# Normed operands for SwiGLU tiles 3 to 21, low halves and adaLN fetches on GpSimd, adaLN steps in singles

## Chip, cores and metric

The kernel runs on one core of a Trainium2 chip. The metric is the device time of one execution in microseconds; the time of a kernel is the median of its runs. The profile is of one further execution, recorded by the hardware profiler.

## What is computed

One inference step of a two-layer backbone on 384 tokens (128 context, 256 latent) of width 1024, all in float32. Each layer is a half SwiGLU feed-forward, a mixer (layer 0: DeltaNet and windowed attention; layer 1: gated linear attention), and a second half SwiGLU. Every sub-layer is normed and modulated by shift and scale, which the adaLN projection makes from a conditioning vector, one for context and one for latent tokens. The change is in the feed-forwards:

```python
def _rmsnorm(x, g):
    y = x * lax.rsqrt(jnp.mean(x * x, axis=-1, keepdims=True) + EPS)
    return y * g

def _modnorm(x, g, shift, scale):
    return _rmsnorm(x, g) * (1.0 + scale) + shift

def _ffn_half(x, mod, i, g, w_gu, w_down):          # w_gu (1024, 2*2816), w_down (2816, 1024)
    h = _modnorm(x, g, mod[:, i], mod[:, i + 1])
    gt, up = jnp.split(h @ w_gu, 2, axis=-1)
    return x + 0.5 * mod[:, i + 2] * ((silu(gt) * up) @ w_down)

def _ada(cond, w, b):                               # nine vectors of 1024 a layer
    return (jax.nn.silu(cond) @ w + b).reshape(cond.shape[0], N_MOD, 1, D_MODEL)
```

## The kernel before

All activations lie transposed: 8 rows of 128 channels, 384 tokens wide. A float32 product is made of three products of rounded operands: weight and activation are each split into a high half (a cast on ScalarE) and a low half (a subtraction on VectorE), and `products` (L189) issues low x high, high x low and high x high for each of the 8 (or up to 6) blocks of a weight tile.

A weight tile goes through `split_w`: a DMA on SP's queue into one of three `w` buffers (L174), a cast to `wh` on ScalarE (L176), a subtraction to `wl` on VectorE (L177). `wh` and `wl` have two buffers each, so one tile's halves can be made while another's are in use.

The norm before a feed-forward is folded into the tiles. `norm_tile` makes `hh` and `hl` from x times the scale alone, without the token's factor 1/rms (`rb`), as soon as a row of x is final, and two further columns hold the shift: an operand is 386 wide. After a projection `scaled` (L203, VectorE) multiplies the result in PSUM by `rb`, and the two last columns, now the shift's share of either stream, are added as a bias: on ScalarE in the SiLU (L332, once per stream), on VectorE in the product of gate and up (L337, once per stream). `rb` itself is ready some microseconds into the first tile (`end_norm`, L300).

`ffn` has two halves of 11 tiles. A tile is a gate and an up projection of 24 matmuls each, the SiLU, the product `a`, and its split into `ah` (ScalarE, L181) and `al` (VectorE, L182). After the 11 tiles come 8 down tiles, each of 33 matmuls over two weight pieces of 6 and 5 blocks (768 and 640 columns), and a `residual` into x (L305, VectorE). In the second half `after(m)` starts the next norm on each finished row. There are four feed-forwards; between the first and second runs the even mixer, between the third and fourth the odd one.

The adaLN vectors for later sub-layers are made beside the feed-forwards, on VectorE: `ada_rows` holds two sum rows per vector (one per stream) and adds eight weight rows to each, one step per row and stream (L145 the first, L147 the others; 16 steps a vector). A weight row of 512 KB is fetched by `ada_tile` (L103) on SP's queue into one of two `aw` buffers, in front of its first step. When a vector is done `ada_sum` has TensorE sum over partitions (L161), and `ada_end` copies and transposes the result into `mod` (L128). `between` draws these steps: two or three after each tile, two after a down tile of the first half, one in the second. Its `issue_after` keeps them behind the given VectorE instruction in VectorE's order. The feed-forwards make 5, 4, 4 and 1 vectors. `side` draws early weight tiles of the following mixer from tile 18 on (first and third feed-forward).

The order in each engine's queue is made by a list scheduler when the program is built: an instruction goes in when its inputs and buffers are ready, earlier program text first. So work whose inputs are ready early can move ahead of its place in the text.

## Time and profile before

| | us |
|---|---|
| median of three runs | 1720.08 |
| lowest, highest | 1715.61, 1723.51 |
| the profiled execution: its own time | 1724.06 |
| the profiled execution: span from the first to the last instruction | 1722.3 |
| TensorE matmul busy in the span | 1656.9 |
| VectorE busy | 1237.5 |
| ScalarE busy | 749.2 |
| GpSimd busy | 0.2 |

PE is TensorE's matmuls, PEld its weight loads, DVE VectorE, ACT ScalarE, POOL GpSimd, SP the engine that issues the DMAs. Busy time is the time in which an engine has an instruction in work; matmuls overlap, so a busy TensorE is not one at its peak. The chain that ended last is followed back from the last instruction: at each step to what released it. An idle time is put down to what ended it.

### The profile page before, as it was taken

What the parts mean: (1) busy time and instruction counts of PE and PEld (TensorE: products, weight loads), DVE (VectorE), ACT (ScalarE), POOL (GpSimd) and SP (SyncE); (2) the same over time, 40 slices, a digit from 0 to 9 for tenths busy, and PEclk for the clock granted to TensorE, in tenths of its full rate; (3) what the DMA queues carried; (4) which work ended last, traced back from release to release, by engine and by line L of the source; (5) the groups of instructions that cost most, each with busy time, mean ns of one, the idle gap of its engine ahead of it and who ended that gap; (6) DMA issues with size and microseconds to landing.
All of it is one profiled execution on the core that took longest, in us unless ns stands there. A gap on an engine that the chain in (4) does not pass through costs nothing.

```text
span 1722.3 us, 26237 instructions
## 1 busy us (share of the span) xinstructions
PE 1656.9 (96%) x10341; PEld 1570.9 (91%) x10341; DVE 1237.5 (72%) x2091; ACT 749.2 (44%) x1301; POOL 0.2 (0%) x4
## 2 busy tenths in 40 slices
PE   5999998999999999999999999999999999999997
PEld 3998998899888899989999998999898889999997
DVE  3887787777868768877856887786567768744554
ACT  4432343366336443323344432344655754433343
POOL 0000000000000000000000000000000000000000
PEclk8999999999999989999999999999999999999998
DMA  8566666451321226666644656574313354434332
GB/s 321 183 186 186 204 205 210 148 188 62 114 78 50 77 84 196 180 198 196 185 132 147 197 187 198 188 228 135 102 62 96 102 172 147 159 111 136 126 110 95
DMA packets 80376, 261.83 MB, mean 152 GB/s; under 512 B 9691, under 2 KB 11739, under 8 KB 80124
## 3 DMA queue, kind: packets, MB, share of 16 engines
q1 hardware_dynamic: 80252, 260.15, 47.8%
q8 instruction: 81, 1.33, 0.3%
q14 instruction: 43, 0.35, 0.1%
HBM read 255.13 MB, written 4.98 MB: 151 GB/s over the span
## 4 chain that ended last, share of the span: by engine, by line
PE 82%; DVE 10%; DMA 4%; issue 2%; ACT 2%; SPq 0%; DVEq 0%; ACTq 0%
PE acc L189 71%; DVE acc L147 3%; DVE wl L177 2%; DMA aw<-in_adaw_dram 2%; PE ada L161 1%; DVE x L305 1%; DMA w<-in_evw_dram 1%; DMA w<-in_wdn_dram 1%; PE ps L679 1%; PE ps L683 1%; PE ada L113 1%; PE ss L289 1%; PE ps L1139 1%; PE ps L647 0%; DVE ssum L276 0%
## 5 line engine op out<-in xcount | busy, mean ns | idle before, releaser
L176 ACT CAST wh<-w 128x1024 fp32r<-128x1024 f32 (+1 forms) x358 | 340.2, 951 | 683.5 <-PE acc L189 491.0
L189 PE MATMUL acc<-hh,wl 128*128 128x386 f32 x1728 | 595.3, 345 | 7.3 <-DVE wl L177 7.2
L189 PE MATMUL acc<-hl,wh 128*128 128x386 f32 x1728 | 589.6, 341 | 0.0
L189 PE MATMUL acc<-hh,wh 128*128 128x386 f32 x1728 | 587.9, 340 | 0.0
L177 DVE TENSOR_TENSOR wl<-w,wh 128x1024 fp32r<-128x1024 f32 (+1 forms) x358 | 392.3, 1097 | 98.3 <-ACT wh L176 96.8
L189 PEld LDWEIGHTS acc<-hh,wl 128*128 128x128 f32 x1728 | 325.6, 188 | 19.4 <-DVE wl L177 9.5
L189 PEld LDWEIGHTS acc<-hl,wh 128*128 128x128 f32 x1728 | 327.2, 189 | 2.3 <-issue 0.8
L189 PEld LDWEIGHTS acc<-hh,wh 128*128 128x128 f32 x1728 | 325.5, 188 | 2.3 <-issue 0.8
L189 PE MATMUL acc<-ah,wl 128*128 128x384 f32 x704 | 242.2, 344 | 17.2 <-DVE wl L177 16.8
L147 DVE SCALAR_TENSOR_TENSOR acc<-aw,cs,acc 128x1024 f32<-128x1024 f32 x196 | 243.1, 1278 | 8.4 <-DMA aw<-in_adaw_dram 8.4
L189 PE MATMUL acc<-al,wh 128*128 128x384 f32 x704 | 238.5, 339 | 0.0
L189 PE MATMUL acc<-ah,wh 128*128 128x384 f32 x704 | 238.4, 339 | 0.0
L189 PEld LDWEIGHTS acc<-ah,wl 128*128 128x128 f32 x704 | 132.7, 189 | 27.9 <-DVE wl L177 27.9
L189 PEld LDWEIGHTS acc<-al,wh 128*128 128x128 f32 x704 | 132.9, 189 | 0.0
L189 PEld LDWEIGHTS acc<-ah,wh 128*128 128x128 f32 x704 | 132.8, 189 | 0.0
L203 DVE TENSOR_TENSOR tu<-acc,rb 128x386 f32<-128x386 f32 x88 | 49.2, 559 | 105.7 <-PE acc L189 105.6
L203 DVE TENSOR_TENSOR tg<-acc,rb 128x386 f32<-128x386 f32 x138 | 76.6, 555 | 55.3 <-PE acc L189 52.0
L305 DVE SCALAR_TENSOR_TENSOR x<-acc,hg,x 128x128 f32<-128x128 f32 (+1 forms) x128 | 47.5, 413 | 68.5 <-PE acc L189 68.5
L332 ACT ACTIVATE sg<-tg 128x128 f32<-128x128 f32 (+1 forms) x176 | 70.6, 448 | 51.6 <-DVE tg L203 51.5
L337 DVE SCALAR_TENSOR_TENSOR a<-tu,sg 128x128 f32<-128x128 f32 (+1 forms) x176 | 65.7, 415 | 8.3
L181 ACT CAST ah<-a 128x384 fp32r<-128x384 f32 x88 | 45.3, 515 | 41.5 <-DVE a L337 41.3
L182 DVE TENSOR_TENSOR al<-a,ah 128x384 fp32r<-128x384 f32 x88 | 48.6, 552 | 3.5 <-ACT ah L181 3.5
(368 smaller groups left out, 1502.4 us busy)
## 6 DMA issues: line engine op xcount, KB each, us to landing
w<-in_wgu_dram SPq DMA_DIRECT2D x176, 512.0 KB, 3.7
aw<-in_adaw_dram SPq DMA_DIRECT2D x144, 512.0 KB, 4.2
w<-in_wdn_dram SPq DMA_DIRECT2D x64, 384.0 KB, 3.1
w<-in_wdn_dram SPq DMA_DIRECT2D x64, 320.0 KB, 3.0
w<-in_evw_dram SPq DMA_DIRECT2D x24, 512.0 KB, 4.1
w<-in_odw_dram SPq DMA_DIRECT2D x24, 512.0 KB, 3.6
w<-in_evo_dram SPq DMA_DIRECT2D x8, 512.0 KB, 3.5
w<-in_odo_dram SPq DMA_DIRECT2D x8, 512.0 KB, 4.0
```

Source lines behind the costliest of these rows:

```text
L113: nc.tensor.matmul(ps[32 * g:32 * g + 32, 0:256], self.cs[:, k, :], w[:, 256 * g:256 * g + 256], start=k == 0, stop=k == KD - 1)
L147: nc.vector.scalar_tensor_tensor(t, w, cs, t, op0=ALU.mult, op1=ALU.add)
L161: self.nc.tensor.matmul(ps[32 * g:32 * g + 32, 0:256], self.pick[:, s], acc[s][:, 256 * g:256 * g + 256], start=s == 0, stop=s == 1)
L176: nc.scalar.copy(wh[:, 0:n], w[:, 0:n])
L177: nc.vector.tensor_tensor(wl[:, 0:n], w[:, 0:n], wh[:, 0:n].bitcast(F32), op=ALU.subtract)
L181: self.nc.scalar.copy(hi, src)
L182: return self.nc.vector.tensor_tensor(lo, src, hi.bitcast(F32), op=ALU.subtract)
L189: self.nc.tensor.matmul(out, s[:, sl], mv[:, k0 + k], start=first and k == 0 and i == 0, stop=last and k == nk - 1 and i == 2)
L203: self.nc.vector.tensor_tensor(t[0:m], p, self.rb[0:m], op=ALU.mult)
L305: i = nc.vector.scalar_tensor_tensor(self.x[:, k, lo:hi], p[:, lo:hi], gate[:, k, s:s + 1], self.x[:, k, lo:hi], op0=ALU.mult, op1=ALU.add)
L332: nc.scalar.activation(sg[:, lo:hi], tg[:, lo:hi], AF.Silu, bias=tg[:, T + s:T + s + 1])
L337: nc.vector.scalar_tensor_tensor(a32[:, lo:hi], tu[:, lo:hi], tu[:, T + s:T + s + 1], sg[:, lo:hi], op0=ALU.add, op1=ALU.mult)
```

## The change

Tiles 0 to 2 of each feed-forward keep the folded form. Beside them the full operand of the norm is made: per row of x a product with `rb` on GpSimd, scale and shift by two ScalarE activations, a cast, and a subtraction on GpSimd (`normed`, `nh` and `nl`, 384 columns). Tiles 3 to 21 read these: the SiLU takes the gate from PSUM in one activation, and `a` is one VectorE product of PSUM and SiLU. The low half `al` is made on GpSimd for all tiles but the last of a half. adaLN weight rows for `ada_rows` are fetched from GpSimd's queue, the sum rows share three buffers for four, and the steps are drawn one after each tile 0 to 2, then `steps/2` behind the gate's weight split and `steps/2` behind the product, with fractions carried over; `steps` is 2.8, 2.4, 2.4 and 2 for the four feed-forwards. Down tiles draw as before.

```diff
--- before.py
+++ after.py
@@ -98,9 +98,9 @@
             self.nc.sync.dma_start(self.x[:, k:k + 2], self.xd[:, k:k + 2])
 
 
-    def ada_tile(self, v, k, pool=None):
+    def ada_tile(self, v, k, pool=None, queue=None):
         w = (pool or self.adar).tile([128, 1024], F32, tag="aw", name=self.name("aw"))
-        self.nc.sync.dma_start(w, self.a["adaw"][v // 2, k, v % 2])
+        (queue or self.nc.sync).dma_start(w, self.a["adaw"][v // 2, k, v % 2])
         return w
 
     def ada(self, v, pool=None):
@@ -136,9 +136,9 @@
         nc = self.nc
         ready = None
         for v in vs:
-            acc = [pool.tile([128, 1024], F32, tag=f"acc{s}", bufs=2, name=self.name("acc")) for s in range(2)]
+            acc = [pool.tile([128, 1024], F32, tag="acc", bufs=3, name=self.name("acc")) for s in range(2)]
             for k in range(KD):
-                w = self.ada_tile(v, k)
+                w = self.ada_tile(v, k, queue=nc.gpsimd)
                 for s in range(2):
                     t, cs = acc[s], self.cs[:, k, s:s + 1]
                     if k == 0:
@@ -174,12 +174,12 @@
         nc.sync.dma_start(w[:, 0:n], src)
         wh, wl = to or [self.ring.tile([128, 1024], F32R, tag=t, bufs=2, name=self.name(t)) for t in ("wh", "wl")]
         nc.scalar.copy(wh[:, 0:n], w[:, 0:n])
-        nc.vector.tensor_tensor(wl[:, 0:n], w[:, 0:n], wh[:, 0:n].bitcast(F32), op=ALU.subtract)
+        self.last_split = nc.vector.tensor_tensor(wl[:, 0:n], w[:, 0:n], wh[:, 0:n].bitcast(F32), op=ALU.subtract)
         return wh, wl
 
-    def split(self, hi, lo, src):
+    def split(self, hi, lo, src, engine=None):
         self.nc.scalar.copy(hi, src)
-        return self.nc.vector.tensor_tensor(lo, src, hi.bitcast(F32), op=ALU.subtract)
+        return (engine or self.nc.vector).tensor_tensor(lo, src, hi.bitcast(F32), op=ALU.subtract)
 
     def products(self, out, w, xh, xl, nk, m, first, last, k0=0):
         wh, wl = w
@@ -189,12 +189,13 @@
                 self.nc.tensor.matmul(out, s[:, sl], mv[:, k0 + k], start=first and k == 0 and i == 0,
                                       stop=last and k == nk - 1 and i == 2)
 
-    def proj(self, src, m=128):
+    def proj(self, src, m=128, h=None):
 
         w = src if isinstance(src, tuple) else self.split_w(src, KD * m)
         p = self.acc.tile([128, 512], F32, tag="acc", name=self.name("acc"))
-        self.products(p[0:m, 0:TC], w, self.hh, self.hl, KD, m, True, True)
-        return p[0:m, 0:TC]
+        n = TC if h is None else T
+        self.products(p[0:m, 0:n], w, *(h or (self.hh, self.hl)), KD, m, True, True)
+        return p[0:m, 0:n]
 
     def scaled(self, p, t=None):
         if t is None:
@@ -307,39 +308,66 @@
         return i
 
 
-    def ffn(self, f, l, gate, after, rows=(), side=iter(()), skip=0):
+    def ffn(self, f, l, gate, after, rows=(), side=iter(()), skip=0, steps=2):
+
+
 
         nc = self.nc
+        gs, shift = self.gs, self.m(l, gate - 2)
         hg = self.small.tile([128, KD, 2], F32, tag="hg", name=self.name("hg"))
         with self.tc.tile_pool(name=self.name("ffn"), bufs=1) as pool:
             ah = pool.tile([128, NF // 2, T], F32R, name=self.name("ah"))
             al = pool.tile([128, NF // 2, T], F32R, name=self.name("al"))
+            h = [pool.tile([128, KD, T], F32R, name=self.name(t)) for t in ("nh", "nl")]
             work = lambda tag, n: pool.tile([128, n], F32, tag=tag, bufs=2, name=self.name(tag))
             rows = self.ada_rows(rows, pool) if rows else iter(())
+            raw, due = 3, 0.0
 
             def between(last, n):
+                nonlocal due
+                due += n
                 with self.tc.issue_after(last.ins):
-                    for _ in range(n):
+                    while due >= 1:
                         next(rows, None)
+                        due -= 1
+
+            def normed(k):
+                t = self.tmp.tile([128, T], F32, tag="xg", name=self.name("nx"))
+                nc.gpsimd.tensor_tensor(t, self.x[:, k], self.rb[:, 0:T], op=ALU.mult)
+                for s, lo, hi in STREAMS:
+                    nc.scalar.activation(t[:, lo:hi], t[:, lo:hi], AF.Identity, bias=shift[:, k, s:s + 1],
+                                         scale=gs[:, k, s:s + 1])
+                self.split(h[0][:, k], h[1][:, k], t, nc.gpsimd)
 
             for half in range(2):
                 for jj in range(NF // 2):
                     j = half * (NF // 2) + jj
-                    pg = self.proj(self.a["wgu"][f, 2 * j])
-                    tg = self.scaled(pg)
+                    hj = None if j < raw else h
+                    pg = self.proj(self.a["wgu"][f, 2 * j], h=hj)
                     sg = work("sg", T)
-                    for s, lo, hi in STREAMS:
-                        nc.scalar.activation(sg[:, lo:hi], tg[:, lo:hi], AF.Silu, bias=tg[:, T + s:T + s + 1])
-                    pu = self.proj(self.a["wgu"][f, 2 * j + 1])
-                    tu = self.scaled(pu, work("tu", TC))
+                    if j < raw:
+                        tg = self.scaled(pg)
+                        for s, lo, hi in STREAMS:
+                            nc.scalar.activation(sg[:, lo:hi], tg[:, lo:hi], AF.Silu, bias=tg[:, T + s:T + s + 1])
+                    else:
+                        between(self.last_split, steps / 2)
+                        nc.scalar.activation(sg, pg, AF.Silu)
+                    pu = self.proj(self.a["wgu"][f, 2 * j + 1], h=hj)
                     a32 = work("a32", T)
-                    for s, lo, hi in STREAMS:
-                        nc.vector.scalar_tensor_tensor(a32[:, lo:hi], tu[:, lo:hi], tu[:, T + s:T + s + 1],
-                                                       sg[:, lo:hi], op0=ALU.add, op1=ALU.mult)
-                    last = self.split(ah[:, jj], al[:, jj], a32)
+                    if j < raw:
+                        tu = self.scaled(pu, work("tu", TC))
+                        for s, lo, hi in STREAMS:
+                            last = nc.vector.scalar_tensor_tensor(a32[:, lo:hi], tu[:, lo:hi], tu[:, T + s:T + s + 1],
+                                                                  sg[:, lo:hi], op0=ALU.add, op1=ALU.mult)
+                    else:
+                        last = nc.vector.tensor_tensor(a32, pu, sg, op=ALU.mult)
+                    self.split(ah[:, jj], al[:, jj], a32, nc.vector if jj == NF // 2 - 1 else nc.gpsimd)
+                    if j < raw:
+                        for k in range(KD * j // raw, KD * (j + 1) // raw):
+                            normed(k)
                     if j >= skip:
                         next(side, None)
-                    between(last, 2 + j % 2)
+                    between(last, 1 if j < raw else steps / 2)
                 if half == 0:
                     nc.vector.tensor_scalar(hg, self.m(l, gate), 0.5, None, op0=ALU.mult)
                 else:
@@ -1177,12 +1205,12 @@
         n.begin_shift(0, 0)
     with tc.tile_pool(name="even_late", bufs=1) as late:
         even = Even(n, o, late, n.norm_after(0, 2, 6, 7))
-        n.ffn(0, 0, 2, n.norm_after(0, 1, 3, 4), (2, 3, 4, 5, 6), even.weights(), 18)
+        n.ffn(0, 0, 2, n.norm_after(0, 1, 3, 4), (2, 3, 4, 5, 6), even.weights(), 18, 2.8)
         even.run(n.ada(7))
-    n.ffn(1, 0, 8, n.norm_after(1, 0, 0, 1), (8, 9, 10, 11))
+    n.ffn(1, 0, 8, n.norm_after(1, 0, 0, 1), (8, 9, 10, 11), steps=2.4)
     with tc.tile_pool(name="odd_late", bufs=1) as late:
         odd = Odd(n, o, late, n.norm_after(1, 2, 6, 7))
-        n.ffn(2, 1, 2, n.norm_after(1, 1, 3, 4), (12, 13, 14, 15), odd.weights(), 18)
+        n.ffn(2, 1, 2, n.norm_after(1, 1, 3, 4), (12, 13, 14, 15), odd.weights(), 18, 2.4)
         odd.run(n.ada(16))
 
     def final(m):
```

## Rows read from the trace of the kernel before

**Rows 1.** The page: busy us by engine, and the chain's shares.
```profile
PE 1656.9 (96%) x10341; PEld 1570.9 (91%) x10341; DVE 1237.5 (72%) x2091; ACT 749.2 (44%) x1301; POOL 0.2 (0%) x4
...
PE 82%; DVE 10%; DMA 4%; issue 2%; ACT 2%; SPq 0%; DVEq 0%; ACTq 0%
```

**Rows 2.** The page's groups: busy us, mean ns, then idle before and its releaser.
```profile
L189 PE MATMUL acc<-hh,wl 128*128 128x386 f32 x1728 | 595.3, 345 | 7.3 <-DVE wl L177 7.2
...
L189 PE MATMUL acc<-ah,wl 128*128 128x384 f32 x704 | 242.2, 344 | 17.2 <-DVE wl L177 16.8
```

**Rows 3.** Stretches: length, busy us of PE, PEld, DVE, ACT, POOL, clock, DMA.
```profile
132.30:185.60 53.30, 49.94 (x283) 46.20 (x282) 38.77 (x51) 13.49 (x18) 0.00 (x0) 1.00 0.64 193
185.60:283.60 98.00, 97.48 (x566) 93.97 (x566) 83.89 (x110) 41.59 (x61) 0.00 (x0) 1.00 0.67 214
283.60:343.00 59.40, 50.21 (x268) 47.80 (x267) 40.95 (x67) 20.76 (x40) 0.00 (x0) 0.94 0.48 152
...
778.50:875.50 97.00, 96.77 (x566) 93.66 (x565) 75.89 (x102) 37.32 (x56) 0.00 (x0) 1.00 0.61 185
1071.70:1169.50 97.80, 97.12 (x567) 93.78 (x566) 81.20 (x105) 42.02 (x61) 0.00 (x0) 1.00 0.64 207
1568.10:1661.30 93.20, 93.20 (x530) 93.20 (x530) 50.45 (x75) 35.77 (x54) 0.00 (x0) 1.00 0.39 123
1661.30:1708.00 46.70, 46.70 (x267) 46.70 (x265) 23.01 (x39) 20.20 (x30) 0.00 (x0) 1.00 0.33 95
931.20:949.55 18.35, 18.35 (x106) 18.19 (x105) 14.69 (x20) 8.73 (x13) 0.00 (x0) 1.00 0.52 169
```

**Rows 4.** The chain from 1490 us on: start us, us, what.
```profile
1494.82 1.00 PE ada L161 x16
...
1496.77 211.30 PE acc L189 x1197
```

**Rows 5.** The page's groups of VectorE and ScalarE that the change touches.
```profile
L147 DVE SCALAR_TENSOR_TENSOR acc<-aw,cs,acc 128x1024 f32<-128x1024 f32 x196 | 243.1, 1278 | 8.4 <-DMA aw<-in_adaw_dram 8.4
...
L203 DVE TENSOR_TENSOR tu<-acc,rb 128x386 f32<-128x386 f32 x88 | 49.2, 559 | 105.7 <-PE acc L189 105.6
...
L332 ACT ACTIVATE sg<-tg 128x128 f32<-128x128 f32 (+1 forms) x176 | 70.6, 448 | 51.6 <-DVE tg L203 51.5
L337 DVE SCALAR_TENSOR_TENSOR a<-tu,sg 128x128 f32<-128x128 f32 (+1 forms) x176 | 65.7, 415 | 8.3
L181 ACT CAST ah<-a 128x384 fp32r<-128x384 f32 x88 | 45.3, 515 | 41.5 <-DVE a L337 41.3
L182 DVE TENSOR_TENSOR al<-a,ah 128x384 fp32r<-128x384 f32 x88 | 48.6, 552 | 3.5 <-ACT ah L181 3.5
```

**Rows 6.** The chain around the first feed-forward's last down half.
```profile
287.40 3.67 DVE acc L147 x3
...
294.50 8.06 PE acc L189 x33
...
302.59 0.74 DVE x L305 x2
...
309.35 0.74 DVE x L305 x2
```

**Rows 7.** TensorE's waits, 283 to 343 us: total us, times, longest us.
```profile
PE acc L189 <- DVE wl L177: 9.2, 7, 4.9
```

**Rows 8.** The page's DMA issues: KB each, median us to landing.
```profile
aw<-in_adaw_dram SPq DMA_DIRECT2D x144, 512.0 KB, 4.2
```

**Rows 9.** Timeline, third feed-forward: `rb` is made; tile 3's first matmul.
```profile
930.71 0.48 ACT L300 COPY rb<-rb 128x384 f32<-128x384 f32 x1 [1.65 <-PE rb L297]
...
949.55 0.44 PE L189 MATMUL acc<-hh,wl 128*128 128x386 f32 x1
```

**Rows 10.** Groups with shapes apart: the splits of a full weight tile.
```profile
L177 DVE TENSOR_TENSOR wl<-w,wh 128x1024 fp32r<-128x1024 f32 x228 | 277.8, 1220 | 30.9 <-ACT wh L176 30.1
...
L176 ACT CAST wh<-w 128x1024 fp32r<-128x1024 f32 x228 | 239.5, 1051 | 429.3 <-PE acc L189 272.0 <-issue 138.5 <-ACT sg L332 11.9
```

## The prediction

> **What bounds the kernel now.** I read the page first: TensorE is busy 96% of the span, and the chain that ended last is 82% TensorE [rows 1]. So an edit is worth what it takes from TensorE's own stream or from its waits. Of the waits the page gives totals by operand: matmuls on `hh` (gate and up tiles, and the mixers' projections) waited 7.2 us for `wl` on VectorE, matmuls on `ah` (down tiles) 16.8 us [rows 2]. 24 us is 1.4% of the run, and that is the prize.
>
> Then the stretches by stage [rows 3]. A gate/up half is 11 x 2 x 24 = 528 matmuls, a down half 264. In the last feed-forward, where adaLN steps run out early, they take 93.2 and 46.7 us: 176.5 and 176.9 ns a matmul. In the three feed-forwards that also do adaLN steps a second gate/up half takes 97.0 to 98.0 us, the first one's first down half 53.3 and its second down half 59.4. The excess over 93.2 and 46.7 is where a lighter VectorE can pay; VectorE is busy 83.9 of 98.0 us there, and 50.5 of 93.2 where nothing is lost.
>
> Last the chain of the final 215 us: 1197 matmuls of both widths in one unbroken piece of 211.30 us, 176.5 ns each [rows 4]. TensorE's floor in these stages is this pace, and nothing else wins while it holds.
>
> **The change, part by part.**
>
> *Two columns fewer.* 4 x 19 x 2 x 24 = 3648 matmuls go from 386 to 384 columns. In proportion that would be 0.9 ns each, 3.3 us. But the 384-column down half ran at 176.9 and the 386-column half at 176.5 [rows 3], so width does not set the pace. I take 0; bounds 0 and -3.3.
>
> *Less VectorE and ScalarE work in tiles 3 to 21.* Per tile VectorE loses two scalings of 0.56, two `a` halves of 0.415 each and one `al` of 0.55, 2.5 us, and gains one product from PSUM, which I price as the scaling it resembles, 0.56. Net 1.9 us of some 8.5 a tile [rows 5]. What hides the cost of the rest is that TensorE has one tile's weights split ahead. The gain lies only where `wl` now comes late. Second gate/up halves: 98.0 + 97.0 + 97.8 - 3 x 93.2 = 13.2 us over the floor. Two vectors end in each of these halves, and a vector's sum on TensorE is 1.00 us [rows 4], which stays: 6.0. That leaves 7.2 us. Steps in singles rather than in twos and threes (each 1.28 us) help the same waits. Some of the rest is the changeover around the sums, so I take -3.5; bounds 0 and -7.2.
>
> *The last down half of the first feed-forward.* 59.4 - 46.7 = 12.7 us. Two things make it. (a) Eight steps are left for it, one behind each residual: a tile's period is 309.35 - 302.59 = 6.76 us [rows 6] against 33 x 0.1765 = 5.82, 0.94 x 7 = 6.6 us. Counted out, the change leaves eight again (72 of 82 calls made by then, against 71), in the same place of VectorE's queue, so this stays. (b) The start: TensorE waits once for 4.9 us [rows 7], since three steps (3.67 us), a residual, a fourth step and two `hl` writes stand before the next `wl`; it restarts slow, 33 matmuls in 8.06 us [rows 6], after that idle wait, in a stretch whose mean granted clock is 0.94, so partly at the lower of its two levels, where the others have 1.00 [rows 3]. With 1.4 steps behind the gate's weights and 1.4 behind the product, and 1.9 us less from the tile, VectorE arrives about 3 us earlier. The wait falls to some 2 us and most of the slow restart (8.06 - 5.82 = 2.2) goes. I take -4.5; bounds 0 and -7.1.
>
> *First down halves (three).* The steps there stay two behind each residual: 2 x 1.28 us between a residual and the next tile's second `wl`. The excess (53.3 - 46.7 = 6.6, one sum in it) stays but for the first tile, which starts from a shorter backlog: -0.5 each, -1.5; bounds +3 and -4.5, if single fetches come late or early.
>
> *Fetches on GpSimd.* 14 vectors x 8 = 112 fetches leave SP, where they stood in order among weight loads and held these back while they waited for one of two `aw` buffers. On SP one takes 4.2 us from issue to landing [rows 8]; GpSimd has issued none. A buffer is free when its second step ends and is needed again three step intervals later: at 2.4 steps in 8.5 us, 3 x 3.5 - 1.3 = 9.3 us; in down halves, in the worse phase, 6.8. A fetch may double and stay hidden in the gate/up halves. Behind a waiting fetch on GpSimd's queue stand the next fetches and `al` writes; who needs `al` is a down half, at least a tile later, and the half's last `al` stays on VectorE. I take 0, inside the bounds of the down halves above.
>
> *Three sum buffers for four.* The second sum row of a new vector now waits until TensorE has summed the old one. Behind it on VectorE stand the weight splits. TensorE does that sum at a tile's edge with the next tile's weights already split, 24 x 0.1765 = 4.2 us of cover against one step of 1.28. 0.
>
> *Making the operands, tiles 0 to 2.* For each of 8 rows of x: one product on GpSimd, two activations and a cast on ScalarE, one subtraction on GpSimd. ScalarE: 2 x 0.45 + 0.515 = 1.41, 11.3 us a feed-forward [rows 5]. All start only when `rb` is there. In the third feed-forward that is 931.2 us, and tile 3 starts at 949.55 [rows 9]: 18.4 us, and 7/8 of a tile's 4.2 us more for the last row, 22.1 in all. ScalarE is busy 8.7 us in that stretch already [rows 3], so 20.0 of 22.1: it fits, if its queue never stands still. It is in order, and an activation waits for GpSimd's product; behind it stand the casts of the weights (1.05), then `wl` (1.22) [rows 10], then TensorE. Of the 4.2 us of cover these two leave 1.9. GpSimd did four memsets in this run and no tensor work [rows 1], so its price P has no row. The same operation on VectorE is 0.55 [rows 5], one 2.7 times as wide 1.22 [rows 10]; I take 0.9, the middle, since neither row is nearer. 18 P (16, and two `al`) is then 16.2 of 22.1 us. The chain of a row, P + 1.41 + P = 3.2 us with two buffers, is 12.8 us for eight. So it fits with little to spare, and I put 1.5 us of lost TensorE time on each of the three feed-forwards that start on a fresh `rb`, none on the first, whose `rb` is made before its first tile: +4.5; bounds 0 and +27 (below).
>
> For P the Trainium skill (GPSIMD Engine Reference, Elementwise side-by-side) has 4497 ns for a two-input add of 2048 fp32 elements; by proportion an estimate for 384 is 0.84 us. No run here shows it; with it the sum would stay as it is.
>
> **Sum.** -3.5 - 4.5 - 1.5 + 4.5 = -5.0 us. The profiled execution took 1724.06 us, 4 us over the median of three (1720.08, from 1715.61 to 1723.51), so it becomes 1719.1; carried to the median, **1715**. A measurement of this kernel tells about 0.5% (8.6 us) from no change.
>
> **Rivals.**
>
> *Slower: the new operands are late at tile 3.* If GpSimd and VectorE can't read together, VectorE's work with two operands in SBUF has to go in turn with GpSimd's: in the stretch of 18.4 us four `wl` (4.9), two `a` (1.7) and two steps (2.6), 9.2 us, and 18 P. This is 9.2 + 22.0 = 31.2 us at P = 1.22, against 22.1: 9 us late, three times, +27. With the gains of -9.5 that is +17.5: **1738**. It decides from P = 1.05 (28.1 us, 6 late, 18 in all, +8.6). At P = 0.9 the loss is 3.3 each and the result about level. For it: the tight sums above; against it: half of VectorE's stretch may slip, and ScalarE alone already spaces GpSimd's work.
>
> The Trainium skill (SBUF — State Buffer, Who interferes with whom) speaks for this rival: VectorE with two SBUF inputs and a GpSimd instruction that reads SBUF share one read interface, and the later one blocks for the whole instruction. No run here shows it, as GpSimd was idle.
>
> *Faster than the forecast.* The operands are made without loss, and the waits go at the far bounds: -7.2 and -7.1 and -1.5: -15.8, **1704**. For it: VectorE then has over 1.9 us a tile to spare, and SP never holds back a weight load. Against it: the sums' changeovers are in these figures.
>
> *The change doesn't reach TensorE.* Only late waits of the start (b) shrink by half and the operands cost that again: **1720**. For it: TensorE is 96% busy already, and the steps behind residuals are untouched.
>
> **How the numbers follow.** Forecast (1709 to 1721) 0.42; operands late 0.23; far bounds 0.25; no effect 0.10. Predicted: 1715. Four in ten of the forecast's share lie near or under 1711.5 in part; I count 0.12 of its 0.42 as faster. Faster by over 0.5%: 0.25 + 0.12 = 0.37. Within: 0.30 + 0.10 = 0.40. Slower: 0.23. The range leaves out half of the slow rival and the end of the fast one: 1702 to 1734.
>
> **What would show it.** Pace of gate/up matmuls in tiles 3 to 21: still 176 to 177 ns, or the first term is wrong. Second gate/up halves at 95 to 97 us; the first feed-forward's last down half near 55; first down halves 52 to 53. ScalarE and TensorE around tiles 0 to 3 of feed-forwards 2 to 4: a wait of TensorE for `nh` or `nl`, or for a `wl` behind a ScalarE that waits for GpSimd, gives the price of the new work; more than 6 us each and the slow rival holds. GpSimd's products against 0.9 us; VectorE's `wl` against 1.22, whose growth would show the shared read. A fetch over 6.8 us with VectorE waiting for `aw` would make the fetch term wrong.

## The result: slower by 5%, 1808 us for 1720

The changed kernel takes 1808.44 us (median; 1800.02 to 1812.46), the kernel before beside it 1719.60: ratio 1.051, interval 1.0462 to 1.0558. The forecast was 1715, its slow rival 1738, its range ended at 1734. It was wrong, in size and in sign. The profiled execution of the changed kernel took 1805.32 us, its span 1803.5.

The page of the changed kernel: busy us by engine, the chain's shares, and the groups (busy us, mean ns, then idle before and what ended it).

```profile
PE 1667.1 (92%) x10341; PEld 1573.4 (87%) x10341; DVE 1170.9 (65%) x1783; ACT 755.3 (42%) x1321; POOL 246.8 (14%) x260
...
PE 34%; issue 3%; DVE 3%; POOL 2%; DMA 2%; ACT 1%; DVEq 0%; ACTq 0%; POOLq 0%
...
L189 PE MATMUL acc<-nh,wl 128*128 128x384 f32 x1216 | 417.8, 344 | 38.6 <-DVE wl L177 38.6
...
L147 DVE SCALAR_TENSOR_TENSOR acc<-aw,cs,acc 128x1024 f32<-128x1024 f32 x196 | 262.0, 1353 | 29.1 <-DMA aw<-in_adaw_dram 29.0
...
L189 PE MATMUL acc<-ah,wl 128*128 128x384 f32 x704 | 242.6, 345 | 25.6 <-DVE wl L177 25.4
...
L189 PE MATMUL acc<-hh,wl 128*128 128x386 f32 (+2 forms) x512 | 180.8, 353 | 26.2 <-DVE wl L177 26.2
...
aw<-in_adaw_dram POOLq DMA_DIRECT2D x112, 512.0 KB, 4.0
```

VectorE has 67 us less to do than before, as meant [rows 1], and TensorE still waits for `wl`: 90.2 us in the three groups against 24.0 [rows 2]. So VectorE was not too full; its queue was in the wrong order or stood still. Steps now wait 29.0 us for `aw`, against 8.4 [rows 5], although a fetch lands no later (4.0 us, 4.2 on SP [rows 8]): something ahead of the landing makes them late.

The stages of the changed kernel: length, busy us of PE, PEld, DVE, ACT, POOL, clock, DMA.

```profile
36.41:141.84 105.43, 97.49 (x547) 94.31 (x548) 69.59 (x66) 43.12 (x70) 35.06 (x35) 0.98 0.51 168
141.84:196.73 54.89, 50.02 (x284) 46.26 (x284) 38.17 (x50) 13.63 (x19) 4.22 (x8) 1.00 0.56 181
196.73:308.96 112.23, 100.72 (x566) 95.74 (x565) 80.11 (x72) 35.81 (x49) 22.33 (x26) 0.97 0.57 191
308.96:368.10 59.14, 51.21 (x275) 47.82 (x275) 38.23 (x62) 21.25 (x39) 1.58 (x3) 0.97 0.48 157
...
814.87:920.68 105.81, 98.73 (x556) 96.03 (x556) 71.28 (x63) 31.72 (x44) 20.65 (x22) 0.97 0.52 173
...
1135.33:1242.89 107.56, 98.61 (x555) 95.21 (x555) 75.63 (x66) 35.70 (x48) 21.14 (x22) 0.97 0.56 188
...
1648.72:1742.06 93.34, 93.34 (x529) 93.34 (x529) 33.02 (x34) 31.14 (x43) 16.42 (x10) 1.00 0.40 121
```

The last line is the last feed-forward's second half: normed operands, low halves on GpSimd, but no steps, and TensorE never waits (93.3 us, 93.2 before [rows 3]). The three second halves with steps take 112, 106 and 108 us where they took 97 to 98.

In all that follows, stages are added up in four sums, each stage reaching from its first matmul to the next stage's first: first gate/up halves (four), second gate/up halves with steps (the first three feed-forwards), first down halves with steps (the same three), and the first feed-forward's last down half. What is left is the mixers, the start and the end.

| profiled span, us | first gate/up x4 | second gate/up x3 | first down x3 | first FFN's last down | all else | span |
|---|---|---|---|---|---|---|
| before | 390.6 | 292.7 | 158.8 | 59.4 | 820.8 | 1722.3 |
| changed | 427.8 | 325.6 | 167.5 | 59.1 | 823.5 | 1803.5 |

So the 81 us are 37 in the first halves (where operands are made and steps are drawn), 33 in the second and 9 in the first down halves. TensorE's waits for `wl` account for 66 of them (90.2 - 24.0). Some 10 of the rest are longer matmuls (PE busy 1667.1 us, 1656.9 before), for which the clock after a wait is the likely cause. After one of 2.2 us, for instance, the fourth feed-forward has this stretch, 23 matmuls in 5.70 us at a mean granted clock of 0.70, part of it at the lower of the two levels (1.2 of 2.4 GHz):

```profile
1514.60:1520.30 5.70, 5.70 (x23) 5.70 (x24) 0.44 (x1) 4.43 (x9) 4.54 (x5) 0.70 0.28 92
```

### The profile page after: what moved, and what is told of

Same layout as the page of the kernel before. It is cut to its first block, busy times and chain, and to the rows that moved or that the text cites. A ratio compares the mean times of both kernels' runs of the same rounds, so it can differ in the third digit from the quotient of the medians.

```text
span 1803.5 us, 26281 instructions
## 1 busy us (share of the span) xinstructions
PE 1667.1 (92%) x10341; PEld 1573.4 (87%) x10341; DVE 1170.9 (65%) x1783; ACT 755.3 (42%) x1321; POOL 246.8 (14%) x260
## 5 line engine op out<-in xcount | busy, mean ns | idle before, releaser
L189 PE MATMUL acc<-nh,wl 128*128 128x384 f32 x1216 | 417.8, 344 | 38.6 <-DVE wl L177 38.6
L189 PE MATMUL acc<-nh,wh 128*128 128x384 f32 x1216 | 414.6, 341 | 0.0
L189 PE MATMUL acc<-nl,wh 128*128 128x384 f32 x1216 | 413.9, 340 | 0.0
L189 PEld LDWEIGHTS acc<-nh,wl 128*128 128x128 f32 x1216 | 231.3, 190 | 51.7 <-DVE wl L177 41.1
L189 PEld LDWEIGHTS acc<-nl,wh 128*128 128x128 f32 x1216 | 231.4, 190 | 0.0
L189 PEld LDWEIGHTS acc<-nh,wh 128*128 128x128 f32 x1216 | 231.1, 190 | 0.0
L189 PE MATMUL acc<-hh,wl 128*128 128x386 f32 (+2 forms) x512 | 180.8, 353 | 26.2 <-DVE wl L177 26.2
L182 POOL TENSOR_TENSOR al<-a,ah 128x384 fp32r<-128x384 f32 x80 | 110.2, 1377 | 521.3 <-ACT ah L181 518.1
L189 PE MATMUL acc<-hl,wh 128*128 128x386 f32 (+2 forms) x512 | 178.4, 349 | 0.0
L189 PE MATMUL acc<-hh,wh 128*128 128x386 f32 (+2 forms) x512 | 177.4, 347 | 0.0
```

The lines of the kernel that those rows point to most:

```text
L182: return (engine or self.nc.vector).tensor_tensor(lo, src, hi.bitcast(F32), op=ALU.subtract)
L189: self.nc.tensor.matmul(out, s[:, sl], mv[:, k0 + k], start=first and k == 0 and i == 0, stop=last and k == nk - 1 and i == 2)
```

## Experiments 1: undo one part of the change

Two theories stood at first. Theory 1: order on the in-order queues, that is, weight casts on ScalarE behind activations that wait for GpSimd, and on VectorE steps ahead of weight splits, some of them waiting for a fetch. Theory 2: GpSimd and VectorE take turns at reading, and VectorE's lengthened instructions are the loss.

Low halves back on VectorE (`u_low`):

```diff
-self.split(ah[:, jj], al[:, jj], a32, nc.vector if jj == NF // 2 - 1 else nc.gpsimd)
+self.split(ah[:, jj], al[:, jj], a32)
```

> The changed kernel with one part undone: the low half of the product of every SwiGLU tile is made on VectorE again; the operands' products and low halves of the first three tiles, and the adaLN fetches, stay on GpSimd. Theory 1 (order on the in-order queues: weight casts stand behind activations that wait for GpSimd in tiles 0 to 2, adaLN steps stand ahead of weight splits and wait for late fetches): the first halves keep their loss of 8.5 to 11.7 us each, and in the second halves the fetches no longer stand behind low halves on GpSimd, which gives back some 10 to 20 us of 33; about 1790 us, 1780 to 1805. Theory 2 (GpSimd and VectorE take turns at reading, and the stretched VectorE instructions are the loss): of 96 tiles' low halves about 84 no longer stretch anything; about 1765 us, 1755 to 1780.

Fetches back on SyncE (`u_fetch`):

```diff
-w = self.ada_tile(v, k, queue=nc.gpsimd)
+w = self.ada_tile(v, k)
```

> The changed kernel with one part undone: the adaLN weights are fetched on SyncE's queue again. Theory 1: the waits of a step for its tile, up to 3.8 us each in front of a weight split, go; the clusters of three steps stay. The three second halves with steps and the first down halves give back 15 to 30 us of some 41; about 1785 us, 1775 to 1795. Theory 2: nothing of the shared reading changes; 1808 us, 1800 to 1812.

Steps in twos and threes behind the tile's last VectorE instruction (`u_steps`):

```diff
-                        between(self.last_split, steps / 2)
...
-                    between(last, 1 if j < raw else steps / 2)
+                    between(last, 2 + j % 2)
```

> The changed kernel with one part undone: all of a tile's adaLN steps, two and three by turns, go behind its last VectorE instruction as before, none behind the gate's weight split. Theory 1: the steps again stand where VectorE has run ahead, but they now wait in bunches for fetches that GpSimd issues late; the second halves give back about a third, some 10 us, and the first down halves come nearer to what they were; about 1795 us, 1780 to 1810. Theory 2: no change of the shared reading; 1808 us, 1800 to 1812.

No normed operands (`u_norm`; every tile goes the way of the first three, and the making is gone; the steps are drawn as in the change):

```diff
-            raw, due = 3, 0.0
+            raw, due = NF, 0.0
...
-                        for k in range(KD * j // raw, KD * (j + 1) // raw):
-                            normed(k)
```

> The changed kernel without normed operands: all 24 tiles of an FFN run on the raw operands with the folded norm as before; low halves and fetches on GpSimd, three sum buffers and single steps stay. It tells where the loss lies. If the making of the operands in the first three tiles costs what the first halves grew by (8.5, 8.5, 11.7 and 8.7 us), the time falls by some 37 us less 2 to 4 us for 386 columns in place of 384; about 1774 us, 1765 to 1785. If the low halves, fetches and steps alone cost all of it (the first halves keep their loss, for they too have low halves on GpSimd), about 1808 us or more, since VectorE has two more instructions a tile.

| | median us | ratio to before, interval | first gate/up | second gate/up | first down | last down |
|---|---|---|---|---|---|---|
| changed | 1808.4 | 1.051, 1.0462 to 1.0558 | 427.8 | 325.6 | 167.5 | 59.1 |
| u_low | 1784.1 | 1.036, 1.034 to 1.038 | 429.3 | 312.3 | 164.5 | 55.0 |
| u_fetch | 1777.5 | 1.0313, 1.0292 to 1.0334 | 440.8 | 302.0 | 162.7 | 54.6 |
| u_steps | 1841.4 | 1.0697, 1.0676 to 1.0718 | 475.5 | 329.5 | 163.1 | 55.9 |
| u_norm | 1836.8 | 1.0637, 1.0588 to 1.0686 | 435.3 | 351.5 | 172.2 | 56.3 |

Theory 2 alone is out: undoing the fetches, which changes no shared reading of operands, gave the most back (31 us). Theory 1 named `u_low` and `u_fetch` rightly, but missed the other two: without normed operands the kernel got 28 us *slower*, with steps in groups 33. No part by itself was the loss; each of these two relieved something the others had made worse. Nor did `u_fetch` only give back: its first halves took 13 us more (440.8 for 427.8), for which these runs show no reason. (A feed-forward has 22 tiles, so `u_low` moved 80 low halves of 88, where its text has 84 of 96.)

## Experiments 2: one part alone

Low halves and fetches both undone (`u_low_fetch`: the two edits above together):

> Two parts undone together: low halves on VectorE and fetches on SyncE's queue; what is left is the normed operands (GpSimd works in the first three tiles only), the single steps and three sum buffers. If the two parts' losses add (24 and 31 us less), 1754 us. If they are one loss seen twice (a fetch on GpSimd is late because it stands behind a low half, and either undoing ends that), 1770 to 1777 us. In both cases the first halves keep 7 to 12 us each over the kernel before, 30 to 45 us in all, since GpSimd's products still stand ahead of the weight casts there; if only the sharing of reads with the low halves had been the loss, 1722 us or less.

Normed operands alone on the kernel before, with steps, fetches and low halves as they were (`b_norm`; that is `u_low_fetch` with the steps drawn as before, and tied to the low half `al`):

> The kernel before with one part alone: normed operands from tile 3 on, made as in the changed kernel (products and low halves of the operands on GpSimd), three sum buffers; steps two and three by turns behind the tile, fetches on SyncE, products' low halves on VectorE. Theory 1: the first halves lose what the casts behind waiting activations cost, 8 to 15 us each and more where two or three steps stand ahead of the weight splits as well; about 1770 us, 1755 to 1790. Theory 2 (only the shared reading): 18 GpSimd instructions a tile group stretch some 20 VectorE instructions by 0.8 us, hidden for the most part; 1725 to 1735 us.

Fetches alone on the kernel before (`b_fetch`), and low halves alone (`b_low`, whose edit this is):

```diff
-                        nc.vector.scalar_tensor_tensor(a32[:, lo:hi], tu[:, lo:hi], ...
+                        last = nc.vector.scalar_tensor_tensor(a32[:, lo:hi], tu[:, lo:hi], ...
...
-                    last = self.split(ah[:, jj], al[:, jj], a32)
+                    self.split(ah[:, jj], al[:, jj], a32, nc.vector if jj == NF // 2 - 1 else nc.gpsimd)
```

> The kernel before with one part alone: the adaLN weights are fetched on GpSimd's queue, where nothing else stands. If a fetch on GpSimd is late only because low halves and products stand ahead of it there (theory 1), the time stays: 1722 us, 1715 to 1728. If a fetch from GpSimd is dear by itself, because its issue has to wait for VectorE or its landing takes longer, steps wait in front of weight splits here too: 1735 to 1755 us.

> The kernel before with one part alone: low halves of the product of gate and up on GpSimd, 80 of 88. Theory 1: VectorE loses 0.55 us a tile and nothing stands behind GpSimd but the down halves; 1718 to 1728 us. Theory 2: each of these instructions lengthens one or two of VectorE's by 0.8 us, in halves where VectorE also has 30 steps of 1.28 us; as much as 2 to 5 us a half with steps, about 1745 us, 1735 to 1755.

| | median us | ratio to before, interval | first gate/up | second gate/up | first down | last down |
|---|---|---|---|---|---|---|
| before | 1722.4 | | 390.6 | 292.7 | 158.8 | 59.4 |
| u_low_fetch | 1782.1 | 1.0346, 1.0315 to 1.0377 | 433.8 | 309.0 | 163.1 | 54.5 |
| b_norm | 1746.9 | 1.0151, 1.0127 to 1.0174 | 430.7 | 288.8 | 158.4 | 53.4 |
| b_fetch | 1726.8 | 1.0027, 1.0017 to 1.0037 | 391.4 | 294.3 | 160.1 | 59.2 |
| b_low | 1898.3 | 1.1021, 1.0994 to 1.1048 | 495.3 | 363.9 | 166.1 | 58.9 |

Low halves and fetches are one loss seen twice: both undone gave no more (1782) than the fetches alone (1777), and with the low halves off GpSimd's queue the fetches on it cost 2 us (1784.1 to 1782.1), no more than the noise, and 4 on the kernel before. A fetch is dear where other work stands on the same queue. Normed operands alone came out between the two theories, with the loss in the first halves (40 us) that theory 1 has, and a gain in the others.

Two results fit no theory. `u_low_fetch` and `b_norm` differ only in how the steps are drawn and what they are tied to, and the changed kernel's way, in singles and tied to the product, cost 35 us (1782.1 - 1746.9). And `b_low`, which takes 0.55 us a tile from VectorE, cost 176 us, where the dearer theory had at most 33.

The diff of `b_low` holds the reason. Steps are tied behind an instruction, `last`. In the kernel before that is the low half `al`; with `al` on GpSimd it became the product `a`, here and in the change alike. VectorE's rows in the kernel before, second feed-forward, second half (start us, us, what, idle before):

```profile
823.68 0.75 DVE L337 SCALAR_TENSOR_TENSOR a<-tu,sg 128x128 f32<-128x128 f32 x2
824.35 1.22 DVE L177 TENSOR_TENSOR wl<-w,wh 128x1024 fp32r<-128x1024 f32 x1
825.48 0.55 DVE L182 TENSOR_TENSOR al<-a,ah 128x384 fp32r<-128x384 f32 x1
825.95 3.67 DVE L147 SCALAR_TENSOR_TENSOR acc<-aw,cs,acc 128x1024 f32<-128x1024 f32 x3
829.54 0.55 DVE L203 TENSOR_TENSOR tg<-acc,rb 128x386 f32<-128x386 f32 x1
830.01 1.21 DVE L177 TENSOR_TENSOR wl<-w,wh 128x1024 fp32r<-128x1024 f32 x1
```

`al` has to wait for ScalarE's `ah`, so the scheduler puts the next weight split between `a` and `al`, and the steps, tied to `al`, come after that split. Tied to `a` they come before it. This is theory 3, the tie. In the changed kernel, third feed-forward, ScalarE's cast, VectorE and TensorE:

```profile
1031.65 1.05 ACT L176 CAST wh<-w 128x1024 fp32r<-128x1024 f32 x1 [2.74 <-PE acc L189]
```

```profile
1031.72 0.56 DVE L363 TENSOR_TENSOR a<-acc,sg 128x384 f32<-128x384 f32 x1 [1.54 <-PE acc L189]
1032.19 4.43 DVE L147 SCALAR_TENSOR_TENSOR acc<-aw,cs,acc 128x1024 f32<-128x1024 f32 x3
1036.55 2.35 DVE L177 TENSOR_TENSOR wl<-w,wh 128x1024 fp32r<-128x1024 f32 x2
```

```profile
1037.81 0.44 PE L189 MATMUL acc<-nh,wl 128*128 128x384 f32 x1 [2.04 <-DVE wl L177]
```

`wh` is ready at 1032.70. VectorE had begun three steps half a microsecond earlier and comes to the split at 1036.55; TensorE waits 2.04 us. The steps may be drawn in singles, but here three stand together all the same: the group tied to the gate's split, long past, can stand anywhere behind it. (Which of the three belong to that group the rows don't tell.)

## Experiments 3: the tie, and the same steps in a better place

The kernel before, with only the tie moved (`b_anchor`; nothing runs on GpSimd):

```diff
-                        nc.vector.scalar_tensor_tensor(a32[:, lo:hi], tu[:, lo:hi], ...
+                        last = nc.vector.scalar_tensor_tensor(a32[:, lo:hi], tu[:, lo:hi], ...
...
-                    last = self.split(ah[:, jj], al[:, jj], a32)
+                    self.split(ah[:, jj], al[:, jj], a32)
```

> The kernel before with one edit: a tile's steps are tied to its last product instruction instead of to the low half of that product, as the changed kernel ties them. Nothing runs on GpSimd. In VectorE's queue the steps then stand ahead of the next gate's weight split: a, step, low half, steps, tg, split, split, where the kernel before has a, split, low half, steps, tg, split. If the place of the steps is what costs (theory 3, the tie): each of six gate/up halves with steps grows by some 15 to 25 us; about 1840 us, 1790 to 1890. If the loss of the low halves on GpSimd (1898 us) is the shared reading (theory 2), this kernel stays at 1722 us, 1715 to 1730.

Low halves on GpSimd, steps kept behind the next gate's split (`b_low_kept`; `last_split` is the `wl` instruction of the last weight tile):

```diff
                     pg = self.proj(self.a["wgu"][f, 2 * j])
+                    if jj:
+                        between(self.last_split, 3 - j % 2)
...
-                    between(last, 2 + j % 2)
+                    if jj == NF // 2 - 1:
+                        between(last, 2 + j % 2)
```

> Low halves on GpSimd as in the run that gave 1898 us, but a tile's steps are drawn behind the next gate's weight split (inside a half), so that they no longer stand ahead of it. Theory 3 (the tie): nearly all of the 176 us go; 1715 to 1740 us. Theory 2 (shared reading): GpSimd's 80 instructions still meet VectorE's; 1840 us or more.

The kernel before, with every step behind a weight split, in down halves too (`b_split`):

```diff
                     pg = self.proj(self.a["wgu"][f, 2 * j])
+                    between(self.last_split, 1)
...
                     pu = self.proj(self.a["wgu"][f, 2 * j + 1])
+                    between(self.last_split, 1 + j % 2)
...
-                    between(last, 2 + j % 2)
...
                         w = self.split_w(self.a["wdn"][f, half, m, :, c0:c1], (c1 - c0) * 128)
+                        between(self.last_split, 1 if half == 0 or c0 else 0)
...
-                    between(last, 2 - half)
```

> The kernel before, without any of the change, with the steps drawn singly behind weight splits: one behind the gate's, one or two by turns behind the up's, one behind each of the two pieces of a down tile in the first half, one behind the second piece in the second half; as many as before in all. If a step costs only where it stands ahead of a split that TensorE will soon want (theory 3): first down halves fall from 53 to some 47 or 48 us, three times 5; second gate/up halves from 97.6 to 94 or 95; the first feed-forward's last down half from 59.4 to 55; about 1695 us, 1685 to 1710. If VectorE is simply too full in these halves: 1722 us, 1715 to 1730.

And for the first halves, normed operands alone with their products and low halves on VectorE (`b_norm_v`; two engines' names differ from `b_norm`):

> The kernel before with the normed operands, made on VectorE instead of GpSimd (products and low halves; 16 instructions of 0.55 us a feed-forward); all else as in the run with the normed operands alone, 1747 us. If the loss of the first halves (4, 11, 13 and 13 us there) is GpSimd's duration and ScalarE's waits for it, they fall to 2 to 5 us each: 1725 us, 1712 to 1738. If it is ScalarE's 11.3 us more in three tiles, or the columns of work as such, it stays: 1745 us or more, and VectorE's 8.8 us more may add to it, up to 1775.

| | median us | ratio to before, interval | first gate/up | second gate/up | first down | last down |
|---|---|---|---|---|---|---|
| b_anchor | 1882.7 | 1.0919, 1.0891 to 1.0946 | 480.0 | 361.6 | 168.1 | 57.2 |
| b_low_kept | 1737.8 | 1.0091, 1.0066 to 1.0117 | 386.8 | 304.4 | 167.3 | 56.2 |
| b_split | 1689.8 | 0.9814, 0.9795 to 0.9834 | 388.1 | 290.0 | 144.2 | 47.8 |
| b_norm_v | 1728.2 | 1.0032, 1.0018 to 1.0045 | 414.2 | 287.6 | 157.8 | 54.2 |

The tie alone, with GpSimd idle, costs 161 us, and keeping the steps behind the split takes 160 of the 176 us off the low halves on GpSimd. What is left there for shared reading, and for the down halves' first tiles, is 16 us, net of what a lighter VectorE and the steps' new place give. Two answers from one edit each, on opposite sides of the same instruction: theory 3 is shown. VectorE and TensorE in `b_anchor`, and two stretches of it (columns as above):

```profile
909.63 0.75 DVE L337 SCALAR_TENSOR_TENSOR a<-tu,sg 128x128 f32<-128x128 f32 x2
910.29 1.28 DVE L147 SCALAR_TENSOR_TENSOR acc<-aw,cs,acc 128x1024 f32<-128x1024 f32 x1
911.49 0.56 DVE L182 TENSOR_TENSOR al<-a,ah 128x384 fp32r<-128x384 f32 x1
911.96 2.48 DVE L147 SCALAR_TENSOR_TENSOR acc<-aw,cs,acc 128x1024 f32<-128x1024 f32 x2
914.35 0.56 DVE L203 TENSOR_TENSOR tg<-acc,rb 128x386 f32<-128x386 f32 x1
914.82 2.36 DVE L177 TENSOR_TENSOR wl<-w,wh 128x1024 fp32r<-128x1024 f32 x2
```

```profile
916.10 0.44 PE L189 MATMUL acc<-hh,wl 128*128 128x386 f32 x1 [2.93 <-DVE wl L177]
```

```profile
904.50:909.00 4.50, 4.50 (x26) 4.50 (x27) 1.14 (x3) 0.00 (x0) 0.00 (x0) 1.00 0.66 232
...
916.10:922.20 6.10, 6.10 (x26) 6.10 (x27) 1.08 (x1) 0.00 (x0) 0.00 (x0) 0.72 0.69 236
```

The same instructions as in the kernel before, the split last instead of second: TensorE waits 2.93 us, and then runs 26 matmuls in 6.10 us at a granted clock of 0.72, where 26 before took 4.50 at 1.00. So this wait cost half as much again behind it (1.60 us).

`b_split` is the other side of this. Its first down half in the second feed-forward, and TensorE's waits in the whole of it (total us, times, longest us):

```profile
744.30:792.10 47.80, 47.80 (x283) 46.80 (x282) 39.44 (x51) 17.61 (x26) 0.00 (x0) 1.00 0.63 207
```

```profile
PE acc L189 <- DVE wl L177: 7.6, 5, 2.7
```

VectorE does the same work in 47.8 us, where the kernel before took 52.8, and TensorE's waits fall from 24.0 to 7.6 us. This kernel beats both others, with none of the change in it.

`b_norm_v` came near its expected total (1728.2 for 1725), but not by the expected stages: without GpSimd the first halves still lose 24 of the 40 us (1, 7, 8 and 8, where 2 to 5 each were expected). ScalarE's waits for the products fall by most, `b_norm` and then `b_norm_v` (total us, times, longest us):

```profile
ACT nx L338 <- POOL nx L336: 33.5, 22, 2.5
```

```profile
ACT nx L338 <- DVE nx L336: 5.2, 7, 1.6
```

So what GpSimd brings, these waits and the shared reading together, is 16 of the 40, net of the work that VectorE took over. The longest waits of TensorE that are left in `b_norm_v`'s first halves, 2.91 us in three of them, are of the order on VectorE. Third feed-forward, ScalarE's cast, VectorE and TensorE:

```profile
947.64 1.05 ACT L176 CAST wh<-w 128x1024 fp32r<-128x1024 f32 x1 [0.92 <-PE acc L189]
```

```profile
946.74 3.67 DVE L147 SCALAR_TENSOR_TENSOR acc<-aw,cs,acc 128x1024 f32<-128x1024 f32 x3
...
953.48 1.22 DVE L177 TENSOR_TENSOR wl<-w,wh 128x1024 fp32r<-128x1024 f32 x1
```

```profile
954.75 0.69 PE L189 MATMUL acc<-nh,wl 128*128 128x384 f32 x1 [2.91 <-DVE wl L177]
```

`wh` is ready at 948.69; three steps, and then the rows' products and low halves, stand ahead of its split. In `b_norm` GpSimd lengthens such a group of steps as well, ahead of a split for which TensorE waits 4.66 us (962.37):

```profile
954.38 6.00 DVE L147 SCALAR_TENSOR_TENSOR acc<-aw,cs,acc 128x1024 f32<-128x1024 f32 x3
```

## Experiments 4: the rest of the loss, in the changed kernel

The tie mended in the changed kernel's gate/up tiles alone (`a_split`):

```diff
                     pu = self.proj(self.a["wgu"][f, 2 * j + 1], h=hj)
+                    between(self.last_split, 1 if j < raw else steps / 2)
...
-                    between(last, 1 if j < raw else steps / 2)
```

> The changed kernel with one edit: the second group of a gate/up tile's adaLN steps is tied to the up projection's weight split instead of to the product; low halves, products and fetches stay on GpSimd, and down halves stay as they are. If the tie is the second half's loss (theory 3), the three second halves with steps fall from 112, 106 and 108 us to 97 to 100, the first halves keep the making of the operands: 1808 less some 30 to 45, about 1770 us, 1755 to 1780. From single parts on the kernel before it would be 1722 + 25 (normed operands) + 16 (low halves) + 4 (fetches) = 1767. If the tie did nothing here, since steps come singly anyway, 1800 us or more.

Twice the time for the operands: `b_norm` with `raw = 6` (`b_norm_6`), and both mended, with the steps of down tiles as in `b_split` (`a_all`):

> The kernel before with the normed operands alone (on GpSimd, as in the run that gave 1747 us), but made over six tiles instead of three and used from tile 6 on. If the loss of the first halves (4, 11, 13 and 13 us) is that ScalarE's and GpSimd's work for eight rows does not fit between the first norm factor and tile 3 (28.8 us from the first product to the last low half in the fourth feed-forward), it shrinks to 0 to 4 us each: about 1715 us, 1706 to 1726. If each row costs its loss wherever it is made (an activation's wait in front of a cast, eight times), it stays: 1740 us or more.

> The changed kernel with both causes mended: every step tied behind a weight split, in down tiles too (one behind each piece), and the operands made over six tiles. Low halves, products and fetches stay on GpSimd. By the single parts: 1690 (steps behind splits on the kernel before) plus 0 to 4 a feed-forward for the operands, 4 for fetches, and 0 to 16 for low halves: about 1705 us, 1688 to 1722. If sharing of reads between GpSimd and VectorE was the greater cause after all, 1750 us or more.

The counterpart of `a_all` without GpSimd: `b_split` with the operands made on VectorE over six tiles (`split_norm`):

> The kernel that gave 1690 us (steps behind splits, nothing on GpSimd) with normed operands from tile 6 on, made over six tiles on VectorE. TensorE waits for hardly anything there (4.1 us between these matmuls), so VectorE's lighter tiles can give nothing more than the two columns: 0 to 2 us for each of eight halves' later tiles, against VectorE's and ScalarE's 20 us more in each first half: 1690 us, 1680 to 1700.

Then one of GpSimd's jobs at a time taken from `a_all`: the operands to VectorE (`a_all_v`), the fetches to SyncE (`a_all_f`).

> The kernel that gave 1758 us (the changed one with all steps behind splits and the operands made over six tiles) with the operands' products and low halves on VectorE; fetches and the tiles' low halves stay on GpSimd. If ScalarE's waits for GpSimd's products, in front of weight casts, are what the first halves still lose (104.8, 110.4, 107.5 and 107.8 us), these fall to 97 to 101 us as with nothing on GpSimd: some 32 us less, 1726 us, 1718 to 1738. If the first halves lose to fetches and low halves on GpSimd, 1750 us or more.

> The same kernel of 1758 us with the adaLN fetches on SyncE's queue; products and low halves stay on GpSimd. If a step's waits of up to 4 us for its weight row, in front of a split, are what is left in the first feed-forward's second half (109.1 us) and in the down halves of the second and third (55.0 and 53.4 us), these fall to 98 and 48 us: some 20 to 25 us less, 1736 us, 1728 to 1748. If those waits come with the steps' rate and not with the queue, 1755 us or more.

| | median us | ratio to before, interval | first gate/up | second gate/up | first down | last down |
|---|---|---|---|---|---|---|
| a_split | 1783.0 | 1.0362, 1.0324 to 1.04 | 435.0 | 308.1 | 168.3 | 54.9 |
| b_norm_6 | 1741.6 | 1.0116, 1.009 to 1.0141 | 419.6 | 289.2 | 160.0 | 54.3 |
| a_all | 1758.1 | 1.0206, 1.0179 to 1.0234 | 430.5 | 303.3 | 157.7 | 48.6 |
| a_all_v | 1727.7 | 1.0024, 1.0012 to 1.0036 | 394.8 | 306.1 | 161.6 | 48.4 |
| a_all_f | 1732.7 | 1.0053, 1.0036 to 1.0069 | 422.4 | 293.9 | 148.5 | 49.8 |
| split_norm | 1698.4 | 0.986, 0.9827 to 0.9892 | 394.8 | 292.5 | 148.1 | 48.5 |

The tie is worth 25 us in the changed kernel, where I expected 30 to 45: the second halves of the second and third feed-forward fell to 99.4 and 98.0 us as expected, the first one's stayed at 110.7. Time before tile 3 is the smaller part of what the operands lack: with six tiles the loss of the first halves went from 40 us to 29, no more. With six tiles and the steps behind splits, moving the operands to VectorE took all of it but a little (430.5 to 394.8; 388.1 in `b_split` without any); in `b_norm_v`, with neither, it took 16 of 40. So what making a row costs depends on the engine that makes it and on where the steps stand. The changed kernel shows GpSimd's part, third feed-forward: ScalarE, GpSimd, VectorE and TensorE.

```profile
987.08 0.99 ACT L338 ACTIVATE nx<-nx,mod,gs 128x128 f32<-128x128 f32 x2 [1.11 <-POOL nx L336]
989.15 0.49 ACT L338 ACTIVATE nx<-nx,mod,gs 128x128 f32<-128x128 f32 x1 [1.09 <-POOL nx L336]
...
990.46 1.03 ACT L176 CAST wh<-w 128x1024 fp32r<-128x1024 f32 x1
```

```profile
988.10 1.02 POOL L336 TENSOR_TENSOR nx<-x,rb 128x384 f32<-128x384 f32 x1
...
991.21 1.00 POOL L336 TENSOR_TENSOR nx<-x,rb 128x384 f32<-128x384 f32 x1
992.17 1.99 POOL L182 TENSOR_TENSOR nl<-nx,nh 128x384 fp32r<-128x384 f32 x1
```

```profile
991.52 1.77 DVE L177 TENSOR_TENSOR wl<-w,wh 128x1024 fp32r<-128x1024 f32 x1 [5.34 <-ACT wh L176]
```

```profile
993.35 0.44 PE L189 MATMUL acc<-hh,wl 128*128 128x386 f32 x1 [2.64 <-DVE wl L177]
```

ScalarE stands twice, 1.1 us each, with the weight cast behind it; VectorE has been idle for 5.34 us when that cast is done; TensorE waits 2.64 us. The rest of VectorE's 5.34 us is ScalarE's own work, for the rows and then the cast (1.03). GpSimd's low half and VectorE's split are both lengthened (1.99 and 1.77 us, alone 1.00 and 1.22), each while the one before it ends on the other engine: the product runs 0.69 us into the split, the split 1.12 us into the low half.

The fetches: VectorE and GpSimd in `a_all`, first feed-forward's second half.

```profile
232.97 3.68 DVE L147 SCALAR_TENSOR_TENSOR acc<-aw,cs,acc 128x1024 f32<-128x1024 f32 x3 [3.98 <-DMA aw<-in_adaw_dram]
236.56 1.22 DVE L177 TENSOR_TENSOR wl<-w,wh 128x1024 fp32r<-128x1024 f32 x1
```

```profile
225.79 1.83 POOL L182 TENSOR_TENSOR al<-a,ah 128x384 fp32r<-128x384 f32 x1 [6.68 <-ACT ah L181]
227.56 0.57 POOL L103 DMA_DIRECT2D aw<-in_adaw_dram  x1
229.00 0.53 POOL L103 DMA_DIRECT2D aw<-in_adaw_dram  x1 [0.86 <-DVE gs L238]
```

The step waits for the fetch of 227.56, which GpSimd issues when a low half of 1.83 us is done; the row lands 5.4 us later, the step has waited 3.98 us, and the split stands behind it. Up to 1.8 us of that wait are the low half ahead of the fetch; the rest these rows don't explain. With fetches on SyncE the first three sums fall by 8, 9 and 9 us.

Together: operands on GpSimd 30 us (1758.1 - 1727.7), fetches on GpSimd 25 (1758.1 - 1732.7), of the 60 between `a_all` and `split_norm`; both came out within 4 us of what was expected of them, while `a_all` itself was expected at 1705, since I had priced the operands on GpSimd by too little time and the fetches by their price alone. By its own sign (1750 us or more) `a_all` spoke for shared reading. Against that, a step takes 1.49 us on average in `a_all`, and still 1.48 in `a_all_v` and `a_all_f` (1.28 before), so these two gave their 30 and 25 us back with VectorE's steps as long as they were. ScalarE's waits for the products fell from 36.4 us to 4.0 in `a_all_v`; how much of them came of GpSimd's own lengthened instructions was not separated. If operands and fetches add, some 4 us are left for the low halves and for the steps' slightly different rates; that was not separated either. (It is not spread evenly: the first feed-forward's second half takes 104.5 us in `a_all_f`, 97.7 in `b_split`.)

## Why the prediction was wrong, point by point

*What bounds the kernel.* Right: TensorE's pace and its waits for `wl`. The floor of these stages held (93.3 us without steps). Wrong was what I drew from it, that a lighter VectorE meets fewer waits. VectorE got 67 us lighter and TensorE waited 66 us longer.

*Gate/up second halves, -3.5.* As a size of the lighter tiles this was right: normed operands alone gave -3.9 (288.8 - 292.7). In the change it was +33. The step that failed is the sentence that steps in singles "help the same waits": I counted the steps and not what they were tied to. The diff showed it (`last` was the low half and became the product), and VectorE's rows of one tile would have shown which instruction stood between. Moving that tie alone cost 161 us on the kernel before; in the changed kernel mending it gave 25 back.

*First feed-forward's last down half, -4.5.* -6.0 with normed operands alone, -0.3 in the change. The reason given (a shorter backlog on VectorE at the start) holds in the one and not in the other: TensorE's wait there, 4.9 us before, is 0.9 with normed operands alone and 3.9 in the change. The 6.6 us of (a) that were to stay did not have to: with the steps behind splits this half took 47.8 us (`b_split`).

*First down halves, -1.5, bounds +3 and -4.5.* -0.4 with normed operands alone, +8.7 in the change. I had put late fetches at +3. And I let the excess of 6.6 us "stay", as if it were VectorE's load: it was the steps' place behind the residual, and one step behind each piece's split took 14.6 us off the three (158.8 to 144.2).

*Fetches on GpSimd, 0.* Alone +4.4 us (1.0017 to 1.0037): near. In the change undoing them gave 31 us, in `a_all` 25. "A fetch may double and stay hidden" looked at its landing, which is 4.0 us. It is the work on the same queue that makes it dear (2 us with the low halves gone, 31 with them), and behind the waiting step stand the weight splits. The prediction asked what stands behind a fetch and not what stands ahead of it.

*Making the operands, +4.5, bounds 0 and +27.* Measured alone +40 in the first halves (430.7 - 390.6), on VectorE +24, and spread over six tiles on VectorE +7 over `b_split`. The mechanism in the text (an activation waits for GpSimd, behind it the cast, then `wl`, then TensorE) is there, but the term is mis-sized: 1.5 us a feed-forward and none in the first, where it measured 11, 13 and 13, and 4 in the first. And it is not all of the term: 24 us of it need no GpSimd. A sum of busy times against a stretch says that work fits; it prices neither eight waits of an in-order queue in front of a cast that has 1.9 us to spare, nor the steps that stand on VectorE between the cast and its split. How the 24 divide between ScalarE's added work and VectorE's order was not separated. The price P was 1.00 us alone (0.9 taken), up to 2.0 beside VectorE.

By proportion from the Trainium skill (GPSIMD Engine Reference, Elementwise — side-by-side cycle accounting) it was 0.84; the trace has 1.00, so that estimate is 16% under it.

*The slow rival, 1738.* It had the right sign and the right engine. Its mechanism, operands late at tile 3, is a part at most: six tiles instead of three took 11 of the 40 us. It left out the tie and the fetches.

The shared read that it drew from the Trainium skill (SBUF — State Buffer, Who interferes with whom) is there: a split of 1.22 us took 1.77 and GpSimd's instruction of 1.00 us took 1.99 in the rows above, while in the last feed-forward's second half, with the same low halves on GpSimd, it cost nothing. With the steps kept behind the split, the low halves on GpSimd cost 16 us net (`b_low_kept`).

*Columns, 0; three sum buffers, 0.* 93.3 us with 384 columns against 93.2 with 386: right for this kernel (but see below). Three buffers were in `b_norm`, whose second halves gained what they should; no run changed them alone.

## What to carry to other kernels

Before moving filler work, write down which instruction it is tied to and what stands between that one and the next instruction that the bottleneck waits for: one instruction earlier in the queue cost 161 us here with no work added, and the same filler behind the weight splits gave 32 us. An idle engine is not a free place when something in order waits for it: price the waits and the work it adds on the other queues (here ScalarE's, with weight casts behind), not its busy time. And undoing parts one at a time doesn't give their prices when they touch one queue: two parts of a change that lost 89 us were worth 28 and 33 us within it.
